# Down projection of a decoder layer: partial products staged by ScalarE and summed in HBM by GpSimd's accumulating DMAs

## The chip, the cores and the metric

One core of a Trainium2 chip runs the whole layer. The time is device microseconds of one launch, as the median of several runs. Engines are named as the profile names them: PE is TensorE, DVE is VectorE, ACT is ScalarE, POOL is GpSimd, SP is SyncE; each works through its own list of instructions in order.

## What is computed

One decoder layer on x of 512 tokens by 2048 channels, in float32: a token mixer in four head groups (a gated delta rule, a linear recurrence, a spatial gating unit, a short convolution) between an input and an output projection, and then the feed-forward that the change is in, with 5632 hidden channels:

```python
        x = x + rms_norm(y, post_mix_norm[l])
        h = rms_norm(x, pre_ffn_norm[l])
        y = conv_ffn(h, ffn_up[l], ffn_conv_w[l], ffn_conv_b[l], ffn_down[l])
        x = x + rms_norm(y, post_ffn_norm[l])

def conv_ffn(h, up, conv_w, conv_b, down):
    hid = causal_dwconv(h @ up.astype(h.dtype), conv_w, conv_b)
    gate, val = jnp.split(hid, 2, axis=-1)
    return (jax.nn.gelu(gate) * val) @ down.astype(h.dtype)
```

## The kernel before

Every product is made three times: weights and activations are each split into a high and a low part (`whi`, `wlo`, for activations `fh`, `fl`), and hi by hi, hi by lo and lo by hi are added up in a PSUM bank (lines 205 to 207). The split of a weight tile is one cast on ScalarE (`whi`, line 155) and one subtraction on VectorE (`wlo`, line 156). The weights come in loads of 512 KB on SyncE's queue (`raw`, line 166), into three buffers; `whi` and `wlo` have four buffers each.

The 5632 hidden channels go in 44 tiles of 128, four to a group, 11 groups. For a group, `up_group` makes four gate and four value tiles (8 tiles of 48 matmuls, PSUM name `pT`), convolves them and multiplies them. Then `down_cols` makes the down projection of the group before: for each of 4 blocks of 512 columns and each of 4 token tiles a product of 128 tokens by 512 columns (`pd`, 12 matmuls), so that a group's burst has 16 tiles. Four PSUM banks take turns: three of tag `acc` and one of tag `fx` (the fourth token tile's), by `bank4`.

The sums over the groups are kept in SBUF, in 16 tiles `facc` of 128 by 512: ScalarE copies the first group's products there, VectorE adds those of the later groups (lines 926 and 928). That is 16 copies and 156 adds: groups 0 to 8 go in whole bursts, group 9 in three column blocks; the last three blocks of group 10, and the fourth block of groups 9 and 10 together, come at the end with `finish` as `after`, which squares, sums, scales and writes out each tile. Ahead of that end the kernel fetches the residual back from HBM (`x1r`, four loads of 1 MB on SyncE's queue, tile name act_hi<-x1d) and four rows of weights (`row`, on ScalarE's queue).

The order of each engine's instructions is set when the program is built, by a scheduler that works on a timeline of its own; buffers of a tag are handed out in program order. Small working tiles (`T`: `fin`, `fcv`, `xr`, `row`, and many in the mixers) have the tag "t" with 10 buffers of 256 KB.

Of the kernel before, what the change touches and what calls it, by code (L numbers as in the profile page):

```python
# [15 lines left out]
P = 128  # L16
S = 512
# [28 lines left out]
# The order in which the mixers' parts are issued: what comes after a part of the DeltaNet fills in  # L46
# where that one waits.
# [9 lines left out]
def trunk(ctx: ExitStack, tc: tile.TileContext, x, xT, cols, rows, gdn_row, sgu_row, w_in, w_ba,  # L57
# [4 lines left out]
    # Slots of one tag are handed out in program order, so work that should run past other work  # L62
    # has tags of its own: G and mm for the DeltaNet, t, acc and fx for what fills in around it.
# [8 lines left out]
    NBUF = {"t": 10, "g": 18, "y": 12, "o": 4, "rb": 1}  # L72
# [10 lines left out]
    def G(name):  # L83
        return new("g", name)
# [10 lines left out]
    def bank4(i):  # L95
        """4 banks that are open at a time."""
        return fx if i == 3 else acc
# [33 lines left out]
    a.activation(out=small([P, 1], "warm"), in_=half[:, 0:1], func=AF.Square)   # its table is loaded early  # L131
# [12 lines left out]
    def split(raw, parts=1, pick=None):  # L144
        """raw [P, 1024], cut along the free axis -> per part (hi, lo)."""
        n = 1024 // parts
        res = []
        for i in range(parts):
            if pick is None:
                hi = wp.tile([P, n], F32R, tag="whi", name="whi", bufs=4)  # L150
                lo = wp.tile([P, n], F32R, tag="wlo", name="wlo", bufs=4)
            else:
                hi, lo = pick("hi"), pick("lo")
            r = raw[:, i * n:(i + 1) * n]
            a.copy(out=hi, in_=r)  # L155
            v.tensor_tensor(out=lo, in0=r, in1=hi.bitcast(F32), op=ALU.subtract)  # L156
            res.append((hi, lo))
        return res

    def load(w, k0, nk, c0, nc_, pieces=1):  # L160
        """nk row tiles of nc_ columns, 1024 elements a partition."""
        raw = wp.tile([P, 1024], F32, tag="raw", name="raw", bufs=3)
        r3 = raw.rearrange("p (k n) -> p k n", n=nc_)
        m = nk // pieces
        for i in range(pieces):
            nc.sync.dma_start(out=r3[:, i * m:(i + 1) * m, :],
                              in_=w[(k0 + i * m) * P:(k0 + (i + 1) * m) * P, c0:c0 + nc_]
                              .rearrange("(k p) n -> p k n", p=P))
        return raw

    def load_cols(w, c0):
        """128 columns, all rows; part (k) -> [P, 128] of hi and lo."""
        h = []
        for i in range(2):
            h += split(load(w, 8 * i, 8, c0, P))
        return lambda k: tuple(t[:, (k % 8) * P:(k % 8 + 1) * P] for t in h[k // 8])

    def load_raw(w, k0, c0, pieces=1):
        """4 row tiles of 512 columns."""
        return [load(w, k0 + 2 * i, 2, c0, S, pieces) for i in range(2)]  # L180

    def split_rows(raws, pick=None):
        """part (i) -> [P, 512] of hi and lo."""
        if pick is not None:
            h4 = sum((split(r, 2, pick) for r in raws), [])
            return lambda i: h4[i]
        h = sum((split(r) for r in raws), [])
        return lambda i: tuple(t[:, (i % 2) * S:(i % 2 + 1) * S] for t in h[i // 2])
# [4 lines left out]
    # One buffer of (hi, lo) activations, [channel, token tile, k, token], for h, y and h2 in turn.  # L193
# [9 lines left out]
    def mul3(p, lt, rt, first, last):  # L203
        """p += lt^T rt of (hi, lo) pairs."""
        pe.matmul(p, lhsT=lt[0], rhs=rt[0], start=first, stop=False)  # L205
        pe.matmul(p, lhsT=lt[0], rhs=rt[1], start=False, stop=False)  # L206
        pe.matmul(p, lhsT=lt[1], rhs=rt[0], start=False, stop=last)  # L207
# [15 lines left out]
    def ones_sum(hi, lo, bank):  # L223
        """sums over the partitions of hi + lo, on every partition."""
        p = bank("psum")
        pe.matmul(p, lhsT=onesr, rhs=hi, start=True, stop=False)
        pe.matmul(p, lhsT=onesr, rhs=lo, start=False, stop=True)
        return p
# [12 lines left out]
    def col_sums(src, bank):  # L241
        """sums over the partitions, tokens on the partitions: [P, token tile]."""
        p = bank("pcs")[:, 0:NTT]
        for t in range(NTT):
            pe.matmul(p[:, t:t + 1], lhsT=src[:, TS[t]], rhs=ones[:, 0:1], start=True, stop=True)
        return p

    def to_row(rc, bank, m=None, tag="t", e=v):
        """[P, token tile] -> the same on every partition, tokens along the free axis (PSUM);
        with m, m^T rc of each token tile."""  # L250
        parts = [sp.tile([P, NTT], F32R, tag=n, name=n) for n in ("rch", "rcl")]
        v.tensor_copy(parts[0], rc)
        v.tensor_tensor(out=parts[1], in0=rc, in1=parts[0].bitcast(F32), op=ALU.subtract)
        dgs = []
        for c in parts:
            dgs.append(new(tag, "dg", F32R))
            e.tensor_tensor(out=blk(dgs[-1]), in0=mid(ident if m is None else m, NTT), op=ALU.mult,
                            in1=c.bitcast(F32).rearrange("p (t o) -> p t o", o=1).broadcast_to([P, NTT, P]))
        return ones_sum(*dgs, bank)

# [1 line left out]
    # lru_x goes along with the rows of x^T as they come  # L262
# [55 lines left out]
    def tanh_gate(t, zh):  # L318
        """zh holds z/2; gives z * sigmoid(z)."""
        th = T("th")  # L320
        a.activation(out=th, in_=zh, func=AF.Tanh)
        v.scalar_tensor_tensor(out=t, in0=th, scalar=1.0, in1=zh, op0=ALU.add, op1=ALU.mult)

    def conv(dst, src, taps, bias=None):
        """causal depthwise convolution along the free axis; taps: columns, oldest first."""
# [28 lines left out]
    def softplus(dst, src, shape):  # L354
        """max(x, 0) + log1p(exp(-|x|)), the logarithm as 2 atanh(u / (2 + u))."""
# [98 lines left out]
    # k and q stay as they are, without their norms. With r = rsqrt(|k|^2 + eps) per token the delta rule  # L454
    # on r k and (beta, v) is the one on k and (beta r^2, v / r): r only scales columns of tokens. The
    # factor of q is one per token of the output and goes into the output's own norm.
    # Both parts of a head are cut into steps, so that the scan of one head can be issued
    # in turn with the preparation of the next.
    def gdn_prep(h, kT, qT, v_s, st):
# [8 lines left out]
        # decays  # L468
# [20 lines left out]
        # k k^T and (q k^T)^T  # L489
# [17 lines left out]
        # natural v  # L507
# [6 lines left out]
        # T = (I + M)^-1 by doubling, as its transpose  # L514
# [19 lines left out]
        # the 32nd power as the 16th's twice  # L534
# [10 lines left out]
        # w^T and u  # L545
# [42 lines left out]
    def gdn_norm(h):  # L588
        """x * rsqrt(mean(x^2) + eps) of x = o * rsqrt(P (|q|^2 + eps))"""
# [23 lines left out]
    def norm4(i, tiles):  # L613
        """rms_norm over 4 channel tiles with the i-th group's weight, in place."""
# [205 lines left out]
    # the last columns by token tile, so that the norm of one runs beside the products of the next  # L820
# [15 lines left out]
    # The first two tiles of the feed-forward go by halves of the tokens, the first half before the  # L836
    # last token tile is there.
# [78 lines left out]
    facc = [[None] * DC for _ in range(NTT)]  # L916

    def down_cols(parts, c, after=None):
        wts = [load_rows(ffn_down, gi * FG, c * S) for gi, _ in parts]
        for t in range(NTT):  # L920
# [3 lines left out]
            if facc[t][c] is None:  # L924
                facc[t][c] = G("facc")
                a.copy(out=facc[t][c], in_=p)
            else:
                v.tensor_tensor(out=facc[t][c], in0=p, in1=facc[t][c], op=ALU.add)  # L928
            if after is not None:
                after(t, c)  # L930
# [48 lines left out]
def _layout(inputs):  # L979
# [4 lines left out]
    def chan(t, n):  # L984
        """[..., n * 128] -> [128, n * ...], the channel within a tile on the partitions."""
# [46 lines left out]
```

## Time and profile before

| | us |
|---|---|
| runs: median (lowest to highest of 3) | 2258.21 (2257.9 to 2258.52) |
| span of the profiled execution, first to last instruction | 2256.1 |
| PE busy, share of the span | 2229.6, 99% |
| DVE busy | 1138.8, 50% |
| ACT busy | 753.2, 33% |
| POOL busy | 104.9, 5% |
| DMA queues' packets, share of 16 engines | 34% |

The mixers run until about 640 us, the output projection until about 820, the feed-forward from there to about 2236, its last norm and the output to the end. The profile's own time for the profiled execution is its span; what lies around the span in a run is the 2.1 us between 2256.1 and the median. Busy shares are of the whole span; how long something takes in the feed-forward is read from stretches of it.

### The profile page before, as it was taken

The page shows a single profiled execution, that of the slowest core. Times are in us where ns is not written, and L with a number is a line of the kernel's source. Part 1 is how long each engine was busy: PE and PEld are TensorE (multiplying, and loading weights), DVE is VectorE, ACT ScalarE, POOL GpSimd, SP SyncE. Part 2 cuts the span into 40 slices and gives each one's busy share as a digit, 9 for nine tenths or more (in the row PEclk, how much of TensorE's full clock was granted, in tenths as well). Part 3 has the DMA queues.
Part 4 walks back from the last instruction along what each step waited for, and adds up shares of the span by engine and source line. Part 5 has one row for each costly group of instructions (what it writes and reads, how often), then busy time and mean ns, then how long its engine had stood idle before and what let it go on. Part 6 is the DMA issues. An engine that isn't in the chain of part 4 may idle for free.

```text
span 2256.1 us, 25143 instructions
## 1 busy us (share of the span) xinstructions
PE 2229.6 (99%) x10260; PEld 1845.3 (82%) x10260; DVE 1138.8 (50%) x1518; ACT 753.2 (33%) x1061; POOL 104.9 (5%) x99
## 2 busy tenths in 40 slices
PE   7999999999999999999999999999999999999998
PEld 6788888888888888888888888888888888888886
DVE  8675453944452474433544445444444444444456
ACT  5464242522332363333223232222323232232323
POOL 6001000100100000000000000000000000000002
PEclk9999999999999999999999999999999999999999
DMA  6222222232243543333333332333333333333352
GB/s 206 72 78 76 66 75 75 78 82 75 84 145 98 168 126 99 94 94 103 90 107 94 96 100 86 106 97 94 103 94 94 98 97 94 103 94 101 96 187 103
DMA packets 308339, 227.13 MB, mean 101 GB/s; under 512 B 8832, under 2 KB 263552, under 8 KB 307712
## 3 DMA queue, kind: packets, MB, share of 16 engines
q1 hardware_dynamic: 303616, 217.15, 33.0%
q10 hardware_dynamic: 4608, 8.39, 1.1%
q8 instruction: 80, 1.31, 0.2%
q14 instruction: 35, 0.29, 0.0%
HBM read 217.12 MB, written 8.39 MB: 100 GB/s over the span
## 4 chain that ended last, share of the span: by engine, by line
issue 63%; PE 31%; ACT 2%; DVE 2%; POOL 1%; DMA 0%; SPq 0%; DVEq 0%; POOLq 0%; ACTq 0%
PE pT L205 5%; PE pT L206 5%; PE pT L207 5%; PE pwo L205 2%; PE pwo L206 2%; PE pwo L207 2%; PE ptt L445 1%; DVE act_lo L280 1%; PE pvs L207 1%; PE pvs L206 1%; PE pvs L205 1%; PE pp L445 1%; PE pss L571 1%; ACT waste L884 0%; DVE wlo L156 0%
## 5 line engine op out<-in xcount | busy, mean ns | idle before, releaser
L205 PE MATMUL pT<-act_hi,whi 128*128 128x512 f32 (+1 forms) x2016 | 781.8, 388 | 1.8 <-ACT act_hi L872 1.8
L206 PE MATMUL pT<-act_lo,whi 128*128 128x512 f32 (+1 forms) x2016 | 781.9, 388 | 0.0
L207 PE MATMUL pT<-act_hi,wlo 128*128 128x512 f32 (+1 forms) x2016 | 780.8, 387 | 0.0
L155 ACT CAST whi<-raw 128x1024 fp32r<-128x1024 f32 x378 | 398.0, 1053 | 1012.3 <-PE pT L206 626.4
L156 DVE TENSOR_TENSOR wlo<-raw,whi 128x1024 fp32r<-128x1024 f32 x378 | 464.5, 1229 | 417.2 <-ACT whi L155 415.7
L205 PEld LDWEIGHTS pT<-act_hi,whi 128*128 128x128 f32 x2016 | 378.5, 188 | 78.9 <-ACT act_hi L872 2.6
L206 PEld LDWEIGHTS pT<-act_lo,whi 128*128 128x128 f32 x2016 | 378.8, 188 | 76.5 <-issue 1.0
L207 PEld LDWEIGHTS pT<-act_hi,wlo 128*128 128x128 f32 x2016 | 378.8, 188 | 76.4 <-issue 1.0
L206 PE MATMUL pd<-wlo,fh 128*128 128x512 f32 x704 | 273.7, 389 | 0.0
L207 PE MATMUL pd<-whi,fl 128*128 128x512 f32 x704 | 273.7, 389 | 0.0
L205 PE MATMUL pd<-whi,fh 128*128 128x512 f32 x704 | 273.5, 389 | 0.0
L315 DVE TENSOR_TENSOR fin<-pT,r2b 128x512 f32<-128x512 f32 x88 | 60.8, 691 | 285.7 <-PE pT L207 285.7
L928 DVE TENSOR_TENSOR facc<-pd,facc 128x512 f32<-128x512 f32 x156 | 107.5, 689 | 132.5 <-PE pd L207 131.8
L206 PEld LDWEIGHTS pd<-wlo,fh 128*128 128x128 f32 x704 | 132.1, 188 | 27.5
L207 PEld LDWEIGHTS pd<-whi,fl 128*128 128x128 f32 x704 | 132.1, 188 | 27.4
L205 PEld LDWEIGHTS pd<-whi,fh 128*128 128x128 f32 x704 | 132.1, 188 | 27.4
L332 DVE SCALAR_TENSOR_TENSOR fcv<-fin,colt,fcv 128x511 f32<-128x511 f32 (+1 forms) x176 | 131.2, 747 | 3.0 <-ACT fcv L330 0.3
L206 PE MATMUL pwo<-wlo,act_hi 128*128 128x512 f32 x224 | 87.1, 389 | 0.0
L207 PE MATMUL pwo<-whi,act_lo 128*128 128x512 f32 x224 | 87.0, 389 | 0.0
L205 PE MATMUL pwo<-whi,act_hi 128*128 128x512 f32 x224 | 86.5, 389 | 0.0
L330 ACT ACTIVATE fcv<-fin,colt 128x512 f32<-128x512 f32 x88 | 71.3, 811 | 1.9 <-DVE fin L315 1.9
L911 ACT CAST fh<-fcv 128x512 fp32r<-128x512 f32 x44 | 27.3, 621 | 122.4 <-DVE fcv L908 122.4
(318 smaller groups left out, 1511.8 us busy)
## 6 DMA issues: line engine op xcount, KB each, us to landing
raw<-in_ffn_up_dram SPq DMA_DIRECT2D x176, 512.0 KB, 4.0
raw<-in_ffn_down_dram SPq DMA_DIRECT2D x88, 512.0 KB, 3.6
raw<-in_w_in_dram SPq DMA_DIRECT2D x86, 512.0 KB, 3.8
raw<-in_w_out_dram SPq DMA_DIRECT2D x32, 512.0 KB, 3.9
xs<-in_xT_dram SPq DMA_DIRECT2D x16, 256.0 KB, 5.3
xr<-in_x_dram ACTq DMA_DIRECT2D x16, 256.0 KB, 5.3
x1d<-yw SPq DMA_DIRECT2D x16, 256.0 KB, 3.6
act_hi<-x1d SPq DMA_DIRECT2D x4, 1024.0 KB, 10.5
```

Source lines behind the costliest of these rows:

```text
L155: a.copy(out=hi, in_=r)
L156: v.tensor_tensor(out=lo, in0=r, in1=hi.bitcast(F32), op=ALU.subtract)
L205: pe.matmul(p, lhsT=lt[0], rhs=rt[0], start=first, stop=False)
L206: pe.matmul(p, lhsT=lt[0], rhs=rt[1], start=False, stop=False)
L207: pe.matmul(p, lhsT=lt[1], rhs=rt[0], start=False, stop=last)
L280: v.scalar_tensor_tensor(out=hl, in0=blk(xs[j]), scalar=col("pre_mix", k), in1=hh.bitcast(F32), op0=ALU.mult, op1=ALU.subtract)
L315: v.tensor_tensor(out=t, in0=p, in1=m, op=ALU.mult)
L330: a.activation(out=dst, in_=src, func=AF.Identity, scale=taps[-1], bias=bias)
L332: v.scalar_tensor_tensor(out=dst[:, j:], in0=src[:, :S - j], scalar=taps[n - 1 - j], in1=dst[:, j:], op0=ALU.mult, op1=ALU.add)
L445: pe.matmul(p[:, TS[t]], lhsT=lhsT[:, TS[t]], rhs=rhs[:, TS[t]], start=True, stop=True)
L911: a.copy(out=ah, in_=vt)
L928: v.tensor_tensor(out=facc[t][c], in0=p, in1=facc[t][c], op=ALU.add)
```

## The change

The 16 sums of the down projection no longer stand in SBUF but in an HBM tensor `fd` of 512 by 2048. ScalarE copies each product of groups 0 to 9 (without the last block) from PSUM to a staging tile `st`, of which there are two. For group 0 a DMA on SyncE's queue writes it to `fd`; for groups 1 to 9 a DMA issued by GpSimd adds it to what stands there. At the end SyncE's queue fetches each of the 16 sums into a tile `facc`, and VectorE adds the last products as before. The two staging buffers are taken from the tag "t", which has 8 instead of 10. Comments went too; they are left out here.

```diff
-    NBUF = {"t": 10, "g": 18, "y": 12, "o": 4, "rb": 1}
+    NBUF = {"t": 8, "st": 2, "g": 18, "y": 12, "o": 4, "rb": 1}
...
     facc = [[None] * DC for _ in range(NTT)]
+    fd = dr.tile([S, D], F32, name="fd")
 
     def down_cols(parts, c, after=None):
...
-            if facc[t][c] is None:
-                facc[t][c] = G("facc")
-                a.copy(out=facc[t][c], in_=p)
+            cs = slice(c * S, (c + 1) * S)
+            if after is None:
+                st = new("st", "st")
+                a.copy(out=st, in_=p)
+                if parts[0][0] == 0:
+                    nc.sync.dma_start(out=fd[TS[t], cs], in_=st)
+                else:
+                    g.dma_start(out=fd[TS[t], cs], in_=st, accum_op=ALU.add)
             else:
+                if facc[t][c] is None:
+                    facc[t][c] = G("facc")
+                    nc.sync.dma_start(out=facc[t][c], in_=fd[TS[t], cs])
                 v.tensor_tensor(out=facc[t][c], in0=p, in1=facc[t][c], op=ALU.add)
-            if after is not None:
                 after(t, c)
```

On ScalarE, at the start of the second group's burst, the casts of the weights follow each other in the kernel before:

```order
L155 CAST whi_8293<-raw_8289 128x1024
L155 CAST whi_8297<-raw_8291 128x1024
L330 ACTIVATE fcv_8212<-fin_8210,colt_75 128x512
L911 CAST fh_8217<-fcv_8212 128x512
L155 CAST whi_8361<-raw_8357 128x1024
L155 CAST whi_8365<-raw_8359 128x1024
L155 CAST whi_8429<-raw_8425 128x1024
L155 CAST whi_8433<-raw_8427 128x1024
```

and in the changed kernel, at the same place:

```order
L155 CAST whi_8318<-raw_8314 128x1024
L155 CAST whi_8322<-raw_8316 128x1024
L330 ACTIVATE fcv_8229<-fin_8227,colt_75 128x512
L928 COPY st_8263<-pd_8250 128x512
L911 CAST fh_8234<-fcv_8229 128x512
L928 COPY st_8279<-pd_8266 128x512
L928 COPY st_8295<-pd_8282 128x512
L155 CAST whi_8394<-raw_8390 128x1024
L928 COPY st_8311<-pd_8298 128x512
L155 CAST whi_8398<-raw_8392 128x1024
L928 COPY st_8339<-pd_8326 128x512
L928 COPY st_8355<-pd_8342 128x512
```

Each copy `st` stands between casts of weights of the columns after it, and from the third on it waits for the DMA of the copy two before it. On GpSimd, all 140 accumulating DMAs stand between its last small operation for the feed-forward's norm and its first of the last norm:

```order
 L141 TENSOR_TENSOR ry<-crs,half 128x1 x4
 L141 TENSOR_TENSOR r_6213<-crs,half 128x4
+L932 DMA fd<-st 128x512 x140
 L141 TENSOR_TENSOR rf<-crs,half 128x1
-L963 TENSOR_TENSOR facc<-facc,act_hi 128x512 x2
+L971 TENSOR_TENSOR facc<-facc,act_hi 128x512 x2
```

GpSimd had nothing to do there. On SyncE's queue, at the end, the loads of weights (`raw`) after those of the residual (`act_hi<-x1d`) were ten in a row:

```order
L166 DMA raw<-in_ffn_down_dram 128x2x512 x6
L945 DMA act_hi<-x1d 128x2048 x4
L166 DMA raw<-in_ffn_down_dram 128x2x512 x10
L967 DMA out_dram<-facc 128x512
L967 DMA out_dram<-fm 128x512
```

and now they have the fetches of the sums between them:

```order
L166 DMA raw<-in_ffn_down_dram 128x2x512 x6
L953 DMA act_hi<-x1d 128x2048 x4
L166 DMA raw<-in_ffn_down_dram 128x2x512 x3
L936 DMA facc<-fd 128x512 x6
L166 DMA raw<-in_ffn_down_dram 128x2x512 x2
L936 DMA facc<-fd 128x512 x4
L166 DMA raw<-in_ffn_down_dram 128x2x512
L936 DMA facc<-fd 128x512
L166 DMA raw<-in_ffn_down_dram 128x2x512
L936 DMA facc<-fd 128x512 x5
L166 DMA raw<-in_ffn_down_dram 128x2x512 x3
```

Six fetches, each of which waits for an accumulating DMA, came ahead of seven loads of weights. PE's list in the feed-forward is the same in both kernels.

## Rows read from the trace of the kernel before

**Rows 1.** The page's head: span, and each engine's busy us (share), instructions

```profile
span 2256.1 us, 25143 instructions
PE 2229.6 (99%) x10260; PEld 1845.3 (82%) x10260; DVE 1138.8 (50%) x1518; ACT 753.2 (33%) x1061; POOL 104.9 (5%) x99
```

**Rows 2.** Busy time by stretches: start:end, length, then as the first line says

```profile
core 0: us, PE busy (x) PEld busy (x) DVE busy (x) ACT busy (x) POOL busy (x), PEclk, DMA share, GB/s
100.00:200.00 100.00, 98.67 (x501) 81.55 (x500) 67.11 (x108) 58.05 (x95) 8.54 (x10) 1.00 0.30 78
700.00:820.00 120.00, 118.72 (x606) 100.81 (x604) 58.31 (x118) 53.17 (x138) 2.20 (x4) 1.00 0.45 143
900.00:2158.00 1258.00, 1258.00 (x5552) 1041.67 (x5551) 585.21 (x676) 359.42 (x406) 0.00 (x0) 1.00 0.34 97
1029.00:1157.00 128.00, 128.00 (x566) 105.98 (x566) 59.46 (x70) 35.01 (x39) 0.00 (x0) 1.00 0.34 99
```

**Rows 3.** The chain of waits in order of time: start us, length us, what

```profile
821.02 1413.07 issue
```

**Rows 4.** Timeline of PE, second group's burst: start us, us, instruction, [idle before]

```profile
1113.59 0.39 PE L205 MATMUL pd<-whi,fh 128*128 128x512 f32 x1
...
1116.31 0.39 PE L205 MATMUL pd<-whi,fh 128*128 128x512 f32 x1
...
1124.47 0.39 PE L205 MATMUL pd<-whi,fh 128*128 128x512 f32 x1
```

**Rows 5.** Evacuations: timeline of DVE there, and the tile facc's copies (min/median/max ns)

```profile
1116.51 0.69 DVE L928 TENSOR_TENSOR facc<-pd,facc 128x512 f32<-128x512 f32 x1
...
L926 ACT COPY facc<-pd x16: 589/589/590, 985.9 to 1026.7; 128x512 f32<-128x512 f32 x16
```

**Rows 6.** Groups on DVE, 1029 to 1157 us: busy us, mean ns, idle before

```profile
L156 DVE TENSOR_TENSOR wlo<-raw,whi 128x1024 fp32r<-128x1024 f32 x23 | 28.1, 1224 | 23.8 <-ACT whi L155 23.8
L332 DVE SCALAR_TENSOR_TENSOR fcv<-fin,colt,fcv 128x511 f32<-128x511 f32 (+1 forms) x16 | 11.9, 747 | 0.2
L928 DVE TENSOR_TENSOR facc<-pd,facc 128x512 f32<-128x512 f32 x15 | 10.3, 690 | 14.3 <-PE pd L207 14.2
L315 DVE TENSOR_TENSOR fin<-pT,r2b 128x512 f32<-128x512 f32 x8 | 5.5, 692 | 26.8 <-PE pT L207 26.8
L908 DVE TENSOR_TENSOR fcv<-fcv 128x512 f32<-128x512 f32 x4 | 2.8, 693 | 0.1
L912 DVE TENSOR_TENSOR fl<-fcv,fh 128x512 fp32r<-128x512 f32 x4 | 2.8, 690 | 2.1 <-ACT fh L911 2.1
```

**Rows 7.** DMA issues of the page: KB each, median us from issue to landing

```profile
raw<-in_ffn_up_dram SPq DMA_DIRECT2D x176, 512.0 KB, 4.0
...
xr<-in_x_dram ACTq DMA_DIRECT2D x16, 256.0 KB, 5.3
x1d<-yw SPq DMA_DIRECT2D x16, 256.0 KB, 3.6
...
out_dram<-facc ACTq DMA_DIRECT2D x8, 256.0 KB, 2.1
```

**Rows 8.** Timeline of POOL: its shortest kind of operation in the last norm

```profile
2234.13 0.55 POOL L141 TENSOR_TENSOR rf<-crs,half 128x1 f32<-128x1 f32 x1 [1413.10 <-DVE crs L140]
```

**Rows 9.** Timeline of SP and of ACT, second burst: a load and its cast

```profile
1125.65 0.37 SPq L166 DMA_DIRECT2D raw<-in_ffn_down_dram  x1
...
1135.59 1.06 ACT L155 CAST whi<-raw 128x1024 fp32r<-128x1024 f32 x1 [0.31 <-PE pd L207]
```

**Rows 10.** Last burst: its first matmul, SP's loads, busy time (as rows 2)

```profile
2158.07 0.39 PE L205 MATMUL pd<-whi,fh 128*128 128x512 f32 x1
...
2158.26 2.08 SPq L945 DMA_DIRECT2D act_hi<-x1d  x4
...
2158.00:2178.00 20.00, 20.00 (x90) 16.55 (x89) 11.61 (x15) 4.50 (x5) 0.00 (x0) 1.00 0.89 341
```

**Rows 11.** The tile row, 2150 to 2230 us: its four loads, and their landing

```profile
L799 ACTq DMA_DIRECT2D row<-in_rows_dram x4: 334/429/860, 2159.0 to 2163.1; - x4
...
DMA to landing us min/median/max: 8.6/13.0/14.8
```

## The prediction

> **What bounds the kernel now.** First the page's head: TensorE (PE) is busy for 2229.6 of 2256.1 us, 99% [rows 1]. The runs shown have a median of 2258.21 us, 2.1 us more than this span; I carry those 2.1 us along unchanged. Then the busy time by stretches: PE lacks 1.3 us in each of 100 to 200 and 700 to 820; from 900 to 2158 us, nearly all of the feed-forward, it is busy without a gap, at a granted clock of 1.00, the 2.4 GHz level: 5552 matmuls in 1258 us, 0.227 us each [rows 2]. The chain of waits says the same: one piece of 1413 us, from 821 us on, in which PE waits for nothing [rows 3]. So in the stage that is edited no wait ends last: the engine itself does. VectorE's 1139 us and ScalarE's 753 us lie beside it [rows 1]. Whatever the edit takes off VectorE there is worth nothing; it can only cost time, by making PE wait.
>
> **What decides whether PE waits.** The order of PE's rows in the feed-forward is the same before and after: eight up tiles, then a burst of 16 down tiles of 12 matmuls. In the burst a new tile begins every 2.72 us (1113.59 to 1116.31) [rows 4]. Four banks rotate, so the first tile's bank is wanted again when the fifth begins, at 1124.47 [rows 4]. Its evacuation began at 1116.51 [rows 5]. A ScalarE copy of that shape takes 0.59 us (the 16 copies of the first group), a VectorE add 0.69 [rows 5]. So a copy may be 1124.47 - 1116.51 - 0.59 = 7.3 us late before PE stops.
>
> **The change, part by part.** VectorE loses 140 adds of 0.69 us, 97 us: worth nothing, as above. ScalarE gets 140 copies more, 0.59 us each, 83 us; in one group's 128 us it now works 35 us [rows 2] and would work 16 x 0.59 more, 44: no bound. PE's order before the feed-forward changes a little, since the ring "t" falls from 10 buffers to 8; PE idles there for 1.3 and 1.3 us [rows 2], and the x rows that are now fetched later take 5.3 us each [rows 7] beside a token tile's 48 matmuls, 10.9 us. I take 0, and plus or minus 1 us.
>
> The price lies in the new ring of two staging buffers. A copy needs the buffer of the copy two before it, so it waits until that one's DMA has landed. Call L the time from the end of a copy to the release of its buffer: the handover, GpSimd's issue, the transfer, the signal. Two copies then take 0.59 + L per buffer, while PE delivers two tiles in 5.43 us. Up to L = 5.43 - 0.59 = 4.84 us nothing is late. Above that each pair falls back by L - 4.84. Tile 11 of 0 to 15 is the last whose bank is wanted in the same burst, after five such steps: PE stops for 5 (L - 4.84) - 7.3, which begins at **L = 6.3 us**. What is queued behind the waiting copy on ScalarE are the casts whi of the next weights, and PE waits for those: the casts for the second up tile stand behind copies 14 and 15, seven steps late, and PE wants them 13.6 us after tile 14 ends; copy (0.59), cast (1.06) and subtraction (1.22) leave some 10.6 us [rows 5, 6, 9], so this stop is 7 (L - 4.84) - 10.6, which begins at 6.35. Both thresholds agree; the second grows faster. There are eight whole bursts with accumulation (128 DMAs) and one of 12 tiles.
>
> No row shows a DMA that GpSimd issues, nor one that adds into HBM, so L is bounded by rows of the same size, 256 KB. From below: a plain write to HBM lands 2.1 us after its issue when nothing else runs [rows 7]. From above: a read from HBM beside the weights, 5.3, and only then a write beside them, 3.6 [rows 7], 8.9, and 0.55 us for the smallest GpSimd instruction [rows 8]: 9.5. An accumulation must fetch its sum before it writes, but the fetch of one partition's row can run beside the write of another's. It is nearest to the 5.3 us read, and with handovers I take **L = 5.5 us**. The lag then is 5 x 0.66 = 3.3 us at tile 11 and 4.6 at tile 14, under 7.3 and 10.6: the covered case, 0 us.
>
> The Trainium skill (DMA: Bandwidth & Descriptors, Anatomy of one DMA) fits such a transfer from GpSimd by 2.0 us plus bytes over 436 GB/s, 2.6 us for 256 KB, an estimate that leaves out the read of the sum; by it nothing would be late at all. No run here shows it.
>
> The weights' own loads, 512 KB each, land in 4.0 us [rows 7]. The second half of the last column's weights is issued at 1125.65 and cast at 1135.59 [rows 9]: 6 us in hand. The DMA engines are 34% busy over a group [rows 2]. I take 0 for that contention outside the last burst.
>
> In the first burst SyncE writes the sums. There the 16 writes stand between loads of weights and each waits for a copy; a write beside weights lands in 3.6 us [rows 7], under 4.84, and the load behind the fourth write of a column has over 20 us until its use. 0 us.
>
> **The last burst is different.** There the four 1 MB loads of x1 start at 2158.3, and the DMA engines are 89% busy until 2178 [rows 10]; four 256 KB loads issued then landed after 8.6 to 14.8 us, median 13.0 [rows 11]. So L is 8.6 or more for the first tiles. Stepped through for L = 8.6 until 2178 and 5.5 afterwards: copies 0 and 1 end at 2161.6 and 2164.65, copies 2 and 3 at 2170.8 and 2173.85, copy 4 at 2180.0, where its bank is wanted at 2158.07 + 8 x 2.72 = 2179.8 [rows 10], copy 5 at 2183.1 against 2182.5, and then each pair falls back 0.65 more until tile 11: PE stops for some 2 us in all. With 13.0 it is copy 2 that ends at 2175.3 against 2174.4, and the sum comes to 2.5 to 6.3 us. If accumulations pass the 1 MB loads at L = 5.5, it is 0. I take 2: the fetches of the sums (16 on SyncE between the last loads of weights) wait for the accumulations two columns back and fit in behind. The finish itself is not edited.
>
> Sum: 2256.1 + 2 (last burst) + 0 (eight bursts) + 0 (rest) + 2.1 = **2260 us**, within the 0.2% (4.5 us) that a measurement of this kernel can tell from no change.
>
> **Rivals.**
>
> 1. L is over 6.35 in every burst, and PE is bound by two buffers: slower. L = 7.0 gives 7 x 2.16 - 10.6 = 4.5 us a burst, 36 in eight, and with some 8 in the last 2302; L = 7.5 gives 8 a burst, 64 and 9, 2331; the upper bound 9.5 gives 22, 176 and 15, 2449. For it: the transfer reads two things and writes one, it is issued on an engine whose shortest instruction takes 0.55 us [rows 8], and two such DMAs are under way beside the weights. Against: the nearest row is a whole microsecond below the threshold, and it takes the mean of a burst, not a single late one.
>
> 2. Only the last burst costs, but more than 4.5 us: L near 13 there [rows 11], and loads of weights that land later behind the accumulations' traffic. 2263 to 2268.
>
> 3. VectorE holds up GpSimd's issue: one subtraction of 1.22 us [rows 6] on top of each L, 6.7 us, is 7 x 1.86 - 10.6 = 2.4 us a burst, 19 in eight: 2279. The rows of one group on VectorE are TENSOR_TENSOR and SCALAR_TENSOR_TENSOR alone, none faster than 1.2 ns for an element of a partition [rows 6]. The Trainium skill (SBUF — State Buffer, Who interferes with whom) warns that GpSimd's writing of descriptors stops while VectorE runs in a two-port mode, as copies, casts and tensor_scalar may, and that tensor_tensor has no such mode; by that rule no instruction listed here would hold it up, and these rows agree as far as they go. 4 in 100, counted in rival 1.
>
> 4. Faster: PE's 2.6 us before the feed-forward vanish by the new order and the last burst costs nothing: 2255.6, still within 0.2%. More than 4.5 us would need the start or the finish to shrink, and neither is edited.
>
> **How the numbers follow.** Forecast (all covered but 0 to 4.5 us in the last burst): 0.52, of which the own range is 2255 to 2263. Rival 2: 0.15. Rival 1 with 3: 0.30, half of it below 2305. Rival 4 beyond 0.2%: 0.03. The range is 2255 to 2305: 0.52 + 0.15 + 0.15 from these cases. Faster 0.03, same 0.52, slower 0.45. The predicted time is the likeliest case's, not the mean.
>
> **What would show it.** Right: the ScalarE copies st begin at most 3 to 5 us after their tile's last matmul; their wait, on GpSimd's DMAs, is long only at the end of a burst; PE stays without a gap from 900 to 2158 us and shows one or two stops between 2174 and 2195. GpSimd's issues land a median of 4.5 to 6 us after they start. Wrong: a median landing of 6 us or more, PE idle in each burst with pd or pT named as waiting for ScalarE (rival 1); stops over 4.5 us after 2174 alone (rival 2); GpSimd's issue taking well over 1 us while VectorE works (rival 3). A stop before 820 us that was not there would say that I took the smaller ring too lightly.

## The result, and the profile after

The changed kernel takes 2270.11 us (median of three runs, 2269.73 to 2271.38) against 2258.21: a ratio of 1.0053, with a 95% interval of 1.0036 to 1.0070. It is slower by 11.9 us. The profiled execution, the slowest of the three, has a span 13.6 us longer than before. The head of its page (span, then each engine's busy us, share and instructions; compare [rows 1]):

```profile
span 2269.7 us, 25613 instructions
PE 2235.1 (98%) x10260; PEld 1848.0 (81%) x10260; DVE 1047.5 (46%) x1378; ACT 824.7 (36%) x1201; POOL 227.3 (10%) x239
```

VectorE has lost 91 us of work, which bought nothing. Where the time went is read from the same stretches as in [rows 2] and [rows 10], TensorE alone (start:end, length, busy us and matmuls, granted clock, DMA share, GB/s):

```profile
core 0: us, PE busy (x), PEclk, DMA share, GB/s
700.00:820.00 120.00, 118.39 (x604) 1.00 0.47 147
900.00:2158.00 1258.00, 1258.00 (x5551) 1.00 0.55 127
2158.00:2180.00 22.00, 20.62 (x92) 1.00 0.94 316
2180.00:2200.00 20.00, 17.26 (x72) 1.00 0.95 227
2200.00:2220.00 20.00, 15.61 (x58) 0.83 0.81 191
```

From 900 to 2158 us there is still no gap: 5551 matmuls, before 5552. The last three stretches in the kernel before:

```profile
2158.00:2180.00 22.00, 22.00 (x99) 1.00 0.82 312
2180.00:2200.00 20.00, 20.00 (x90) 1.00 0.36 106
2200.00:2220.00 20.00, 20.00 (x90) 1.00 0.25 79
```

They held 99, 90 and 90 matmuls, and hold 92, 72 and 58 now. That is 57 fewer, at 0.227 us each 12.9 us, nearly all of the loss. A count by stretches can be off by a matmul or two at their edges. By the timelines it is 12.5 us: the last matmul of `pd` starts at 2258.36 instead of 2244.88, 13.5 us later, and 1.0 us of this was there before the first stop (2175.83 against 2174.84). Most of that 1.0 us is a later start: the second group's burst begins at 1114.34, before at 1113.59 [rows 4]. The named waits of TensorE after 2158 us are one row (us, times, longest); on the timeline they stand ahead of five matmuls, of which three are shown (start, length, instruction, [idle before, releaser]):

```profile
PE pd L205 <- ACT st L928: 8.5, 5, 5.3
```

```profile
2179.64 0.50 PE L205 MATMUL pd<-whi,fh 128*128 128x512 f32 x1 [1.38 <-ACT st L928]
...
2187.28 0.50 PE L205 MATMUL pd<-whi,fh 128*128 128x512 f32 x1 [1.14 <-ACT st L928]
...
2204.39 0.80 PE L205 MATMUL pd<-whi,fh 128*128 128x512 f32 x1 [5.32 <-ACT st L928]
2204.98 0.63 PE L206 MATMUL pd<-wlo,fh 128*128 128x512 f32 x1
```

The waits are 8.5 us of the 12.5. Another part follows the longest of them: after 5.32 us of idling TensorE's matmuls start every 0.43 us instead of every 0.227. The same columns as above, in pieces of 4 us:

```profile
2204.00:2208.00 4.00, 3.61 (x9) 0.50 0.79 147
2208.00:2212.00 4.00, 4.00 (x16) 0.82 0.64 121
2212.00:2216.00 4.00, 4.00 (x20) 1.00 0.80 219
```

The granted clock was 0.50, the 1.2 GHz level, and came back by 2212. The twelve matmuls from 2204.39 on take until 2209.58, 5.2 us in place of 2.7, so the lower clock costs 2.5 us. Some 1.5 us are left. The first matmul behind a stop takes 0.50 us, and the next one starts 0.34 us after it (2179.98) instead of 0.227, so I put them down to the five restarts.

Why the copies were late is read from ScalarE's and SyncE's timelines of the last burst (ScalarE's copies are those of tiles 2, 3, 8 and 9):

```profile
2174.31 0.59 ACT L928 COPY st<-pd 128x512 f32<-128x512 f32 x1 [3.12 <-DMA fd<-st]
2179.00 0.59 ACT L928 COPY st<-pd 128x512 f32<-128x512 f32 x1 [4.10 <-DMA fd<-st]
...
2195.25 0.59 ACT L928 COPY st<-pd 128x512 f32<-128x512 f32 x1 [1.97 <-DMA fd<-st]
2203.75 0.59 ACT L928 COPY st<-pd 128x512 f32<-128x512 f32 x1 [7.91 <-DMA fd<-st]
```

```profile
2159.25 2.06 SPq L953 DMA_DIRECT2D act_hi<-x1d  x4
...
2174.29 18.70 SPq L936 DMA_DIRECT2D facc<-fd  x6
2193.08 0.90 SPq L166 DMA_DIRECT2D raw<-in_ffn_down_dram  x2
2195.17 16.53 SPq L936 DMA_DIRECT2D facc<-fd  x4
```

Copies 0 and 1 ended at 2162.6 and 2165.6, so their buffers came free after L = 11.7 and 13.4 us, beside the four loads of x1 issued at 2159.25. From tile 2 to tile 6 L then falls from 7.6 to 5.3 us. Then copy 7's accumulation takes 10.5 us (its copy ended at 2193.3, copy 9 begins at 2203.75): that is where SyncE fetches the finished sums back and two loads of weights stand between. So two suspects: **X**, the loads of x1, for the first four stops (3.2 us), and **F**, the fetches of the sums, for the fifth. The frame for both is **R**: a late DMA matters only because the ring has two buffers. Its rival is **D**: the DMA engines themselves are short in this stretch (share 0.94 and 0.95), whatever the ring.

### The profile page after: what moved, and what is told of

Same layout as the page of the kernel before. It is cut to its first block, busy times and chain, and to the rows that moved or that the text cites. A ratio compares the mean times of both kernels' runs of the same rounds, so it can differ in the third digit from the quotient of the medians.

```text
span 2269.7 us, 25613 instructions
## 1 busy us (share of the span) xinstructions
PE 2235.1 (98%) x10260; PEld 1848.0 (81%) x10260; DVE 1047.5 (46%) x1378; ACT 824.7 (36%) x1201; POOL 227.3 (10%) x239
## 4 chain that ended last, share of the span: by engine, by line
issue 50%; PE 38%; POOL 6%; DVE 2%; ACT 2%; DMA 1%; SPq 0%; POOLq 0%; DVEq 0%; ACTq 0%
PE pT L205 8%; PE pT L206 8%; PE pT L207 8%; POOL fd L932 5%; PE pwo L206 2%; PE pwo L205 2%; PE pwo L207 2%; PE ptt L445 1%; PE pvs L207 1%; PE pvs L206 1%; PE pvs L205 1%; PE pp L445 1%; DVE act_lo L280 1%; PE pss L571 1%; DMA fd<-st 0%
## 5 line engine op out<-in xcount | busy, mean ns | idle before, releaser
L932 POOL DMA_DIRECT2D fd<-st x140 | 121.1, 865 | 1268.7 <-ACT st L928 1261.5
L928 ACT COPY st<-pd 128x512 f32<-128x512 f32 x156 | 91.7, 588 | 318.3 <-DMA fd<-st 266.0
```

The source lines that it names most:

```text
L928: a.copy(out=st, in_=p)
L932: g.dma_start(out=fd[TS[t], cs], in_=st, accum_op=ALU.add)
```

## The experiments

All ratios are against the kernel before, on the same chip.

**Many staging buffers.** The staging tiles come from a pool of 18 that stands empty until the end.

```diff
-                st = new("st", "st")
+                st = new("g", "st")
```

> The staging tiles come from the pool g of 18 buffers, which stands empty until the last sums come; all else as in the changed kernel (270 instead of 2258). Theory R (the ring of two turns late DMAs into stops of TensorE): ScalarE's copies no longer wait for a DMA, the five stops of 8.5 us after 2160 us and the fall of the granted clock behind them are gone, 2258 to 2261 us. Theory D (the DMA engines, 88% busy and more from 2160 to 2204 us, are what is short; the ring only shows it): the copies don't wait, but the sums or the weights come late and TensorE stops for VectorE's adds or for casts instead, 2264 to 2270 us.

Measured: 2258.51 us, ratio 1.0004 (0.9995 to 1.0013): no difference from before. TensorE has no gap (columns as before), although the DMA share is as high as in the changed kernel or higher, and the twelve accumulations land later, not sooner (GpSimd's DMAs on the tile fd, 2158 to 2236 us; the changed kernel's row first):

```profile
2158.00:2180.00 22.00, 22.00 (x99) 1.00 0.93 307
2180.00:2200.00 20.00, 20.00 (x90) 1.00 1.09 266
2200.00:2220.00 20.00, 20.00 (x90) 1.00 0.81 289
```

```profile
DMA to landing us min/median/max: 4.9/7.0/13.0
...
DMA to landing us min/median/max: 6.3/10.6/13.2
```

D falls as a cause of the loss: transfers that take 10.6 us cost nothing when no copy waits for them. One half of it is true, though. With a deeper ring each accumulation takes longer. In the whole bursts (900 to 2158 us) they land here after a median of 6.3 us, with two buffers after 5.4 (the row stands further down). So L is no constant of the DMA: it changes with the depth of the ring. The smaller ring "t", which is still 8 here, costs nothing that shows either.

**Three staging buffers.** One tile of that pool joins the two (`ring[len(used) % 3]`); nothing else.

> A third staging tile (one buffer of the pool g); loads and fetches as in the changed kernel. Theory R: with three buffers a copy is late only from L = 3 x 2.72 - 0.59 = 7.6 us on, and by L - 7.6 for three tiles; at L of 8.6 to 10 that is under 7.3 us in twelve tiles, so there is no stop and 2258 to 2261 us. Theory D (with more transfers in flight each takes longer): L grows with the third buffer, stops of 3 us or more stay, 2263 to 2268 us.

Measured: 2259.08 us, ratio 1.0005 (0.9996 to 1.0014). One wait is left:

```profile
PE pd L205 <- ACT st L930: 0.9, 1, 0.9
```

R holds: one more buffer of 256 KB takes away the whole loss that can be measured, although these accumulations, too, land later than with two buffers (median 7.9 us in the last burst).

**No fetches.** The sums are written but never read back.

```diff
-                    nc.sync.dma_start(out=facc[t][c], in_=fd[TS[t], cs])
-                v.tensor_tensor(out=facc[t][c], in0=p, in1=facc[t][c], op=ALU.add)
+                v.tensor_tensor(out=facc[t][c], in0=p, in1=pf[c], op=ALU.add)
```

> Leaves out the reading back of the sums: the last 16 adds take a row tile in their place, so the first ten groups don't enter the output; the accumulations themselves are all made. Theory F (the fetches hold up the accumulations): the stop of 5.3 us and the low clock behind it vanish, 3.2 us of stops stay, 2261 to 2264 us. Theory X (the loads of x1 and the lag that they leave): the copies wait as before, 2267 to 2270 us.

Measured: 2264.07 us, ratio 1.0030 (1.0019 to 1.0042). The early stops stay, the late one and the lower clock are gone:

```profile
PE pd L205 <- ACT st L928: 2.8, 4, 1.5
```

So F is worth some 5.5 us of the 12, and X with all else that is left (the later start among it) some 6.5, restarts included.

**The fetches ahead of the last burst.** Group 9's tiles are not staged; the sums of groups 0 to 8 are fetched earlier and VectorE adds both last groups in SBUF (the burst of group 9 takes the branch with `facc`).

> The twelve tiles of the last burst (group 9) are no longer staged: the sums of groups 0 to 8 are fetched ahead of that burst, and VectorE adds groups 9 and 10 to them in SBUF. Eight bursts stay as in the changed kernel. If the last burst alone is what the change costs, as both X and F say, this is 2257 to 2260 us, with no wait of TensorE for ScalarE after 2160 us; if some of the 12 us came from the first eight bursts or the smaller ring t, that part stays: 2262 us or more.

Measured: 2263.16 us, ratio 1.0027 (1.0017 to 1.0037); by the time alone the second expectation, by the rows neither. TensorE has no wait after 2160 us, as in the first, but two new ones in the burst of group 8, which has none in the changed kernel, and 1.2 GHz behind the second:

```profile
PE pd L205 <- ACT st L928: 4.3, 2, 3.3
```

```profile
2071.43 0.50 PE L205 MATMUL pd<-whi,fh 128*128 128x512 f32 x1 [3.33 <-ACT st L928]
...
2072.48 0.63 PE L206 MATMUL pd<-wlo,fh 128*128 128x512 f32 x1
```

SyncE now fetches 16 sums from 2037.6 to 2097 us, beside group 8's accumulations. No load of x1 is near (they are issued at 2165.9). That is F by itself, in another place. The first seven bursts, staged as in the changed kernel, have no wait, so no part of the loss came from them.

**The loads of x1 later, first try.** They stand behind the last group's first column in the program.

> The four 1 MB loads of x1 are issued after the last group's first column instead of before it, some 35 us later; ring of two as in the changed kernel. Theory X (those loads begin the lag: three tiles late, and never caught up): the stops of 3.2 us between 2179 and 2194 us vanish, and with the lag gone the one of 5.3 us at 2204 too, 2258 to 2262 us. Theory F (the fetches of the sums, six issued in a row by SyncE, hold up the accumulations beside them): the 3.2 us vanish but a stop of about 5 us with the lower clock stays, 2264 to 2268 us.

Measured: 2270.77 us, ratio 1.0059 (1.0047 to 1.0072). It tells nothing on X: what sets SyncE's order left the loads where they were, behind the last up tile and ahead of the weights:

```profile
2158.71 2.10 SPq L978 DMA_DIRECT2D act_hi<-x1d  x4
```

**The loads of x1 later, held by data.**

```diff
+        if c == 0:
+            v.tensor_copy(act_hi[:, t, 0, 0:1], fm[:, 0:1])
+            nc.sync.dma_start(out=x1r[t], in_=x1d[TS[t], :])
```

The loads at their old place are taken out.

> The four loads of x1 are held until VectorE has multiplied the first column's tile of the same tokens (by one column that it writes into their place), so they start after 2195 us, when the accumulations are over; ring of two. Theory X+F, two causes that add: the stops between 2179 and 2194 us go, those by the fetches of the sums (6 to 7 us with what follows them) stay: 2263 to 2265 us. Theory X alone (F has its effect only because the copies are late already): no stop at all, 2258 to 2260 us. Theory F alone: 2268 to 2271 us.

Measured: 2269.28 us, ratio 1.0047 (1.0033 to 1.0061). By the time alone this would be F's, but the rows say more. Until 2182 us TensorE runs without a gap, so X's own stops are gone (99 matmuls from 2158 to 2180, as before). But the fetches start sooner (2171.1) and stop it from then on, and the loads of x1, issued from 2214 on, meet other fetches:

```profile
PE pd L205 <- ACT st L928: 4.6, 3, 2.0
PE pd L205 <- DVE facc L937: 2.4, 1, 2.4
```

**The fetches later.** One column of each of eight `facc` tiles is written from the last staged tile, so that their fetches, and the four behind them in SyncE's queue, wait for its copy.

> The fetches of the first two columns' sums are held until ScalarE has copied the last staged tile (by one column that VectorE writes into their place), and stand behind all accumulations but the last; the loads of x1 stay; ring of two. Theory X+F: the stop of 5 us and the low clock behind it go, the stops of some 3 us between 2179 and 2194 us stay, 2262 to 2265 us, as where the fetches were left out. Theory X alone: 2268 to 2271 us. Either may pay 1 to 2 us more if twelve fetches at once come too late for the first adds.

Measured: 2271.85 us, ratio 1.0059 (1.0046 to 1.0071), which by the time alone would speak for X. The rows don't: the waits for copies fell to 3.3 us, near the 2.8 with no fetches, and the stop of 5 us is gone; but twelve fetches at once, issued from 2204.5, came too late for the first add, by more than I had allowed:

```profile
PE pd L205 <- DVE facc L941: 4.1, 1, 4.1
PE pd L205 <- ACT st L930: 3.3, 5, 1.5
```

**Both later.**

> Both of these at once: loads of x1 and fetches of sums held until the accumulations are over; ring of two. Theory X+F: no wait of TensorE for ScalarE after 2160 us, 2257 to 2260 us; 1 to 2 us more if the twelve fetches come too late for the first adds. If the accumulations of the last burst were slow for another cause than these transfers, stops of several us stay: 2262 us or more.

Measured: 2265.57 us, ratio 1.0032 (1.0019 to 1.0044). By the time alone this is the other branch (2262 us or more), but its stops aren't there: no wait for a copy is left, only the late fetch and, behind it, the lower clock (0.72 from 2206 to 2212 us).

```profile
PE pd L205 <- DVE facc L941: 3.9, 1, 3.9
```

Waits for copies in the last burst are thus 8.5 us with X and F, 2.8 with X alone, 4.6 with F alone, 0 with neither. The 4.6 is with the fetches at other times than in the changed kernel, so the parts need not add up exactly. None of the places tried for these transfers was free with two buffers: moved, they cost elsewhere.

**No addition.** GpSimd's DMAs write instead of adding, so only group 9's product comes back from HBM.

```diff
-                    g.dma_start(out=fd[TS[t], cs], in_=st, accum_op=ALU.add)
+                    g.dma_start(out=fd[TS[t], cs], in_=st)
```

> The 140 DMAs of GpSimd write the partial products without adding them, so that only the tenth group's product comes back from HBM and groups 0 to 8 don't enter the output. Theory A (it is the addition, a read and a write in HBM, that makes L long): they land in 3 to 4 us, as SyncE's writes of the first burst do (3.3), the copies in the whole bursts wait little, and in the last burst L is short enough that the stops fall to 0 to 4 us in all: 2258 to 2264 us. Theory I (GpSimd's issue makes L long): landing stays above 5 us and the time at 2267 to 2272 us.

Measured: 2260.53 us, ratio 1.0011 (1.0001 to 1.0020), with one named wait of 2.0 us. In the eight whole bursts (900 to 2158 us) GpSimd's DMAs show on its tile fd (issue ns, then landing us) and in their queue (packets, MB, share of 16 engines). The changed kernel:

```profile
L932 POOL DMA_DIRECT2D fd<-st x128: 853/862/1083, 1118.2 to 2081.5; - x128
...
DMA to landing us min/median/max: 4.3/5.4/7.9
```

```profile
q0 software_dynamic: 18432, 33.56, 20.5%
```

And without the addition:

```profile
L932 POOL DMA_DIRECT2D fd<-st x128: 539/542/782, 1117.8 to 2072.5; - x128
...
DMA to landing us min/median/max: 2.6/3.2/6.9
```

```profile
q0 software_dynamic: 10240, 33.56, 7.1%
```

Theory A holds: the addition lengthens the landing from 3.2 to 5.4 us, counted from the start of the issue, and nearly triples the time on the DMA engines for the same bytes. Theory I is left with the 0.3 us by which the issue is longer.

**How thin the cover is.** In the changed kernel's trace I take the mean L of a burst from the starts of copies 0 and 14: seven buffer turns, less a copy. The second and the fifth group's burst:

```profile
1117.25 0.59 ACT L928 COPY st<-pd 128x512 f32<-128x512 f32 x1 [1.17 <-PE pd L207]
...
1163.24 0.59 ACT L928 COPY st<-pd 128x512 f32<-128x512 f32 x1 [2.70 <-PE pT L206]
...
1508.93 0.59 ACT L928 COPY st<-pd 128x512 f32<-128x512 f32 x1 [1.18 <-PE pd L207]
...
1557.95 0.59 ACT L928 COPY st<-pd 128x512 f32<-128x512 f32 x1 [4.16 <-DMA fd<-st]
```

(1163.24 - 1117.25) / 7 - 0.59 = 5.98, and 6.41. The eight bursts have 5.9 to 6.4, mean 6.06, where the forecast's threshold is 6.3. The fifth group's is the only one above it, and the only one in which TensorE's side waited for a copy at all, a weight load for 0.4 us; its matmuls lost some 0.2 us. To test that threshold I made L longer. The first try makes each accumulation of two DMAs of 256 columns.

> Each accumulation is made by two DMAs of 256 columns, so that GpSimd issues twice; ring of two, and the order of the other engines in the whole bursts as in the changed kernel. There the mean L of the eight bursts was 5.9 to 6.4 us (from the starts of copies 0 and 14), against the 6.3 us from which TensorE stops. Theory R (thin cover): L rises by 0.5 to 0.9 us, so every burst stops by 7 (L - 4.84) - 10.6, for L = 6.5 to 6.9 some 1 to 4 us, half as much again for the restart and the clock; 8 to 46 us in eight bursts and some more in the last, 2278 to 2320 us, TensorE named as waiting for the copies in each burst. If the cover is wider than that sum says, or two halves land as soon as one whole, the bursts stay without a gap and the time at 2267 to 2274 us.

Measured: 2274.00 us, ratio 1.0074 (1.0057 to 1.0091). The expected rise didn't come: two halves land as soon as a whole, the mean L stays at 5.9 to 6.2, and no whole burst has a named wait, as the second branch says. It doesn't test the threshold, but its rows give the count for a covered stretch. The second try puts work ahead of each DMA:

```diff
+                    for h in range(2):
+                        g.tensor_tensor(out=st[:, TS[h]], in0=st[:, TS[h]], in1=ones, op=ALU.mult)
                     g.dma_start(out=fd[TS[t], cs], in_=st, accum_op=ALU.add)
```

> Ahead of each of its 140 accumulations GpSimd multiplies two blocks of 128 x 128 of the staged tile by one, in place; nothing else is changed, and the order of TensorE and ScalarE in the whole bursts stays. This makes L longer by these two instructions, an estimate of 1.0 to 1.6 us by its instructions of 0.55 to 1.5 us elsewhere. Theory R (the bursts are covered by 0.3 us of L only): L of 7.0 to 7.5 us makes every whole burst stop by 7 (L - 4.84) - 10.6, some 4.5 to 8 us, half as much again with the restart and the clock; 8 x 4.5 to 8 x 12, 36 to 96 us on top of the changed kernel, 2306 to 2366 us, TensorE named as waiting for the copies in each burst. If the cover is wider than that sum says, the bursts stay without a gap and the time under 2280 us.

Measured: 2285.97 us, ratio 1.0129 (1.0112 to 1.0145). The halves first, then the delay, by stretches that hold one burst each:

```profile
1110.00:1240.00 130.00, 130.00 (x575) 1.00 0.62 130
```

```profile
1110.00:1240.00 130.00, 128.38 (x564) 1.00 0.58 126
...
1760.00:1890.00 130.00, 130.00 (x576) 1.00 0.59 130
```

The mean L of each burst, from its copies 0 and 14 as above, against the matmuls that are missing (575 less the row's count, by 0.227 us; the last stretch is longer, 631 of 641). The row between them is the largest lag of copies 0 to 11: how much later a copy starts than copy 0 and 2.72 us a tile (copy 11 of the first: 1157.80 - 1118.00 - 11 x 2.72 = 9.9). These are the copies whose banks the same burst wants again, and the prediction lets them be 7.3 us late.

| burst of group | 1 | 2 | 3 | 4 | 5 | 6 | 7 | 8 |
|---|---|---|---|---|---|---|---|---|
| mean L, us | 6.61 | 6.35 | 6.45 | 6.60 | 6.39 | 6.16 | 6.64 | 6.53 |
| largest lag, us | 9.9 | 7.9 | 8.5 | 9.1 | 8.2 | 7.1 | 8.8 | 9.4 |
| lost, us | 2.5 | 0.7 | 1.4 | 2.0 | 0.9 | 0 | 1.6 | 2.3 |

The one burst below 6.3 loses nothing, all above it lose, which agrees with the threshold. The lag shows the mechanism itself: what a burst loses is its lag less 7.3 us, within 0.2 us in all eight. In the changed kernel the largest lags are 4.5 to 6.6 us, and 7.4 in the fifth group's burst, the one that lost 0.2 us. All eleven named waits of the delayed kernel's whole bursts are for banks; none is for a cast, the other path of the forecast:

```profile
PE pd L205 <- ACT st L928: 6.1, 11, 1.0
```

The time is below what was expected because L rose by 0.4 us on the mean, though the two multiplications take 0.47 us each. A part of the difference is that the accumulations now land sooner, after a median of 5.1 us instead of 5.4. Why the rest is missing stays open; so does why the halves land no later.

**One staging buffer.** `"st": 1` in place of 2.

> One staging tile instead of two. Theory R: a copy then needs the DMA of the copy just before it, so a tile takes 0.59 + L in place of 2.72 us. With L of 4.5 to 5.5 us in the bursts a burst of 16 tiles takes 82 to 98 us instead of 43.5, of which 10.6 are covered: 28 to 44 us a burst, eight times, some 25 to 35 in the last and 20 in the first; 2530 to 2700 us, with TensorE named as waiting for the copies in every burst. If the bursts were covered for another cause than the two buffers (the DMA landing in time for any ring), 2270 to 2300 us.

Measured: 2457.3 us (a single run; before 2257.75). TensorE waits in every burst, a turn takes 5.67 us (16 copies from 1119.94 to 1205.05), so L is 5.1 us with one transfer under way (its median landing 4.8 us):

```profile
PE pd L205 <- ACT st L928: 135.9, 71, 4.8
```

The direction is R's, the size, 200 us, is less than the 270 or more expected. The expectation kept TensorE's order. But with one buffer up tiles of the next group stand among the down tiles (40 triples of their matmuls between 1163 and 1206 us), which probably covers a part; no run tests that.

## Why the prediction came out as it did

The range held the time, the likeliest case didn't: it was 2260 us and no difference that can be told, with 2263 as its end, and the measured loss is clear of the noise. No case of the prediction gives 2270. Rival 2 ends at 2268, and the range goes on to 2305 only for rivals 1 and 3, whose stops in every burst did not come. That the range held is luck. Step by step:

- **The bound, the worthless adds, the eight bursts.** Right. VectorE's 91 us bought nothing, and TensorE's row for 900 to 2158 us is the same. Of the two paths that gave the threshold, the delayed kernel shows the first, 7.3 us until a bank is wanted again. The second, by the casts, was to grow faster; no matmul of the whole bursts waits for one.
- **L = 5.5 us in those bursts.** Too small. Landing is 5.4 us, but with the handover and the spread from burst to burst L is 5.9 to 6.4, and the lag at tile 11 is 4.4 us in the second group's burst (1151.59 against 1117.25 + 11 x 2.72) instead of 3.3. "A whole microsecond below the threshold" was 0.3 us on the mean; in the fifth group's burst L was over it. The result was right by less than the text says, and rival 1 deserved no smaller chance than it got.
- **The rivals on GpSimd's issue.** The issue took 853 to 1083 ns beside VectorE, median 862, so VectorE didn't hold it up by a subtraction's 1.22 us. The Trainium skill (SBUF — State Buffer, Who interferes with whom) says so of tensor_tensor; this trace agrees. The Trainium skill's estimate of 2.6 us for such a transfer (DMA: Bandwidth & Descriptors, Anatomy of one DMA) is near the 3.2 us of the plain writes; the addition, which it leaves out, makes 5.4.
- **The first burst, the weights, the ring "t".** Right as 0: SyncE's writes landed in 3.3 us, no wait for weights shows, and the kernel with many staging buffers and the ring of 8 equals the one before.
- **The last burst, 2 us: the step that failed.** It cost 12.5. Three things in it: (a) beside the x1 loads L was 11.7 and 13.4 us, the 13.0 of [rows 11] and not the 8.6 that I took; stepped through with 13 the text itself has 2.5 to 6.3, and 3.2 were named waits. (b) That the fetches of the sums "fit in behind" is wrong: each is issued as soon as the accumulation into the same sum has landed (the first at 2174.3, just as copy 2 begins), beside the accumulations still to come. It holds these up, and TensorE stops for 5.3 us. Leaving the fetches out gave back 5.5 us. (c) No term stood for what follows a stop: restarts, and 1.2 GHz behind the long one, together some 4 us.
- **Rival 2** had place, sign and most of the cause (the last burst alone, stops of more than 4.5 us after 2174, L near 13, later transfers behind the accumulations' traffic) but ended at 2268, as (b) stood in it for weights only and (c) not at all.

## What to carry to other kernels

A staging ring turns DMA time into engine time only beyond its slack: write down the turn per buffer, n x period less the copy, and set the worst landing in the busiest stretch against it, not the median. Measure that landing with the ring that you will use: here it grew with the ring's depth. Even so, a third buffer was enough, while the DMA engines stayed as busy as with two. When a change sends data out to HBM, look for the place where it comes back: here the return trip met the last of the outgoing. And add to a stop of TensorE what follows it: here some 0.3 us for each restart, and 2.5 us at half the clock behind the longest.

## What the hardware showed that was not expected

- An accumulating DMA of 256 KB costs GpSimd 0.86 us of issue against 0.54 for a plain write, lands in 5.4 against 3.2 us (medians, with two buffers), and takes 20.5% instead of 7.1% of the DMA engines' time for the same 33.56 MB, in 18432 instead of 10240 packets.
- Two accumulations of 128 KB land together as soon as one of 256 KB (mean L 5.9 to 6.2 us against 5.9 to 6.4), although they are issued one after the other at 1.04 us each.
- An accumulation of 256 KB lands later the more of them may be under way: a median of 4.8 us with one staging buffer, 5.4 with two, 6.3 with many.
- TensorE idled for 5.32 us and came back at 0.50 of its clock, the 1.2 GHz level, for about 5 us. After a stop of 3.33 us (the fetches ahead of the last burst) it also fell, with 0.63 us matmuls a microsecond after the restart. So it did after a single stop of 2.24 us in the kernel with halves, while one of 2.03 us in the kernel without the addition, and those of up to 1.5 us in the kernel without fetches, left it at 1.00. The stretches behind the 2.24 and the 2.03 us (columns as before):

```profile
2176.70:2180.70 4.00, 3.97 (x10) 0.57 1.09 362
...
2196.00:2200.00 4.00, 3.99 (x18) 1.00 0.76 232
```
